# Forget sums by way of device memory and GpSimd's mask instead of TensorE's products, in a two-layer sparse-attention trunk

## The chip, the cores and the metric

The kernel runs on one core of a Trainium2 chip. A core has five engines with their own instruction streams: TensorE (PE; its weight loads are shown apart as PEld), VectorE (DVE), ScalarE (ACT), GpSimd (POOL) and SyncE (SP), which here issues all transfers between device memory and the on-chip memory. The metric is the device time of one execution in microseconds (us), the median of several.

## The reference

Two layers, each a mixing part and a squared-ReLU MLP with sandwich RMSNorm, on 256 tokens of 1024 features. The mixing part has 8 NSA heads (compressed, selected and windowed attention) and 8 FoX heads of 64 features. The change touches the FoX heads alone:

```python
log_f = jax.nn.log_sigmoid(f_logits + f_bias)
cum = jnp.cumsum(log_f, axis=1).transpose(0, 2, 1)
for i in range(s // Q_BLOCK):
    q0, q1 = i * Q_BLOCK, (i + 1) * Q_BLOCK
    logits = (einsum('bhqd,bhkd->bhqk', q[:, :, q0:q1], k[:, :, :q1]) * scale
              + cum[:, :, q0:q1, None] - cum[:, :, None, :q1])
    mask = jnp.arange(q1)[None, :] <= jnp.arange(q0, q1)[:, None]
    p = _masked_softmax(logits, mask)
    outs.append(einsum('bhqk,bhkd->bhqd', p, v[:, :, :q1]))
```

The term that depends on the query alone falls out of the softmax, so a kernel needs only the sum at each key, the same for every query row of a head.

## The kernel before

All 256 tokens are held on chip: features or queries on the 128 partitions (rows of the on-chip memory), two query tiles of 128. Weights stream in once as tiles of up to 512 KB into a ring of raw buffers (`raw`, RBUFS = 8). Each is split into a rounded part `whi` (by ACT, some by POOL) and a remainder `wlo` (by DVE), and products are made as hi·hi, hi·lo and lo·hi. The compression weights of the NSA heads (`w`, from `in_cmp_w_k`, `in_cmp_w_v`) use the same ring without a split.

No order of engines is written out by hand. The Python code calls every operation through a recorder, which keeps the operation with the tiles it reads and writes, gives it a key (its place in the listing, or that of its step in a lane) and an estimated cost, and then plans. The planner goes through a list schedule several times, with due times worked out backwards, tries shifts of the order, judges each plan with simulated lateness, and emits the best: the order of each engine's queue, SP's too, is fixed there. A change of one operation's cost, of a buffer count or of a place in the listing can thus change the order of everything.

The mixing part of a layer runs over 24 entries in steps: 16 NSA entries (pair of heads, parity, selected or windowed branch) at steps 0 to 15, then 8 FoX entries (pair, parity) at steps 16 to 23. At a step, `scores` makes the score products for a pair of heads in one stretch of half-array products (64 of the 128 array rows for each head, side by side) and, per entry and query tile, one DVE instruction that adds a mask from SBUF to the scores in PSUM, writes the result and takes the row minimum of the negated, scaled scores. ACT then exponentiates; the next step scales (by POOL for the windowed branch); a step later TensorE turns the probabilities. Between these, `fill` lists the projection products that keep TensorE busy. Jobs in the list `side` are listed at given steps.

The forget sums: `evac1` turns the gate columns into the tiles `lf` (by `absz` and `minz`). `forget_sums`, at step 13, multiplies `lf` by a triangle of ones (`tri`) in PSUM, ACT copies the result as a rounded part (`cumh`), and two DVE instructions make `cum`, which holds rounded parts and remainders in alternating groups of 32 rows. In `fox_scores`, a product with `selr`, which picks the rows of one head, puts the sums of 384 key columns into the score tile for each of the two heads of a pair, and the key products are added on top. The mask added by DVE is then `causal`, the same for all heads.

```python
nc.tensor.matmul(ps[par][:, 0:384], selr[h, i:i + 1].to_broadcast([HD, P]), T["cum"][h],
                 start=True, stop=False, skip_group_check=True)
nc.vector.tensor_tensor_reduce(
    out=p[:, a:b], in0=ps[t], in1=causal[:, S - (b - a):], op0=OP.add, op1=OP.min, ...)
```

In the trace most instructions carry the line of the emitting loop, so they are told apart by the names of their tiles: `s<-cum,selr` the products of the sums, `s<-fkT,fqT` the key products, `s<-tri,lf` the forget sums, `pr<-s,causal` the masked row minimum, `pr<-pr,st,gate` the scaling on POOL.

Of the kernel before, what the change touches and what calls it, by code (L numbers as in the profile page):

```python
# [18 lines left out]
F32 = mybir.dt.float32  # L19
F32R = mybir.dt.float32r  # L20
AF = mybir.ActivationFunctionType
OP = mybir.AluOpType
PSUM = bass.MemoryType.PSUM

P = 128
D = 1024
# [12 lines left out]
SEQ = range(6, 14), range(4, 12)  # L39
SIDE = (6,11), (4, 9)  # L40
PV1 = 15, 14
AFTER = True
PAIRS = False, False
EVKEY = 1
# [4 lines left out]
XAT, PAT = 2, 9  # L49
FIRSTS = [(0, 1), (1, 2), (2, 3), (3, 4), (4, 5), (5, 6), (6, 8)]  # L50
UPK = 7
TOK, WBUFS, RBUFS = 6, 7, 8
LOAD_LEAD, SPLIT_LEAD = 12, 1
OPERANDS = ("whi", "wlo", "xT", "act0", "act1", "qT", "kx0", "kx1", "raw", "gain", "tok", "rl",
            "pr", "prT", "x0", "x1", "fV", "cum", "cs", "pcT", "vbig", "vS", "vW", "kstk", "kstv", "rT", "rCS")
# [8 lines left out]
SEGS = ((0, 128, 0), (128, 384, 1))  # L64
GELU_C = 1.5957691216057308

C_SID, C_CM, C_M01, C_ROW, C_SEL, C_LOW, C_END = np.cumsum([0, 32, 32, 32, 8, 8, 1]).tolist()


def rotation():  # L70
# [5 lines left out]
def constants():  # L76
    c = np.zeros((P, C_END), np.float32)
    i = np.arange(P)
    for t in range(NT):
        ok = (16 * np.arange(16) + 31)[None, :] <= (i + t * P)[:, None]  # L80
        c[:, C_CM + 16 * t:C_CM + 16 * t + 16] = np.where(ok, 0.0, NEG)
        c[:, C_M01 + 16 * t:C_M01 + 16 * t + 16] = ok
    for h in range(8):
        c[16 * h:16 * h + 16, C_ROW + h] = 1.0
        for r in range(0, P, 32):
            c[r + h, C_SEL + h] = 1.0
    for m in range(32):
        c[m::32, C_SID + m] = 1.0
    c[32:64, C_LOW] = c[96:, C_LOW] = -1.0
    return c  # L90


# [34 lines left out]
class Buf:  # L127


    def __init__(self, pool, shape, dtype, name, tag, bufs, psum):  # L130
        self.pool, self.shape, self.dtype, self.name, self.tag, self.bufs = pool, shape, dtype, name, tag, bufs
        self.psum, self.real = psum, None
        self.size = int(np.prod(shape[1:]))
        self.writes, self.reads, self.ops = [], [], 0


class View:
# [14 lines left out]

    def rearrange(self, pattern, **sizes):
        return self._with(lambda ap: ap.rearrange(pattern, **sizes), ix=_regroup(self.ix, pattern, sizes))

    def to_broadcast(self, shape):
        return self._with(lambda ap: ap.to_broadcast(shape), ix=np.broadcast_to(self.ix, shape[1:]))
# [415 lines left out]
def _cost(op, views):  # L573
    out = op.args[0] if op.args else op.kw["out"]
    n = int(np.prod(out.shape[1:]))
    if op.engine == "sync":
        v = views[0][1]
        return v.shape[0] * int(np.prod(v.shape[1:])) * 4 / 320.0
    if op.engine == "tensor":
        if op.name == "stretch":  # L580
            if op.args[2][0][0] == "transpose":
                return 108.0 * len(op.args[2])

            tiles = [_shape(x[1][1]) for x in op.args[2]]
            return sum((x[1][0].ix.size / (2.4 if x[1][1].dtype == F32R else 0.6) + 20) / (P // min(t))
                       for x, t in zip(op.args[2], tiles)) + RETILE * sum(a != b for a, b in zip(tiles, tiles[1:]))
        if op.name == "transpose":
            return 83.0 if op.args[1].dtype == F32R else 108.0
        if op.args[1].dtype == F32R:
            return 13.6 + n / 2.4  # L590
        return max(220.0, 3 + n / 0.6)
    if op.engine == "gpsimd":
        return {"memset": 150, "affine_select": 250}.get(op.name, 400) + (2.1 if op.name == "tensor_scalar" else 1.0) * n
    if op.engine == "vector":
        if op.name == "reciprocal":
            return 60 + 6.5 * n
        if op.name == "tensor_reduce":
            n = int(np.prod(op.args[1].shape[1:]))
        fast = op.name in ("tensor_copy", "tensor_scalar", "memset") and not any(v.buf.psum for _, v in views)
        aps = sum(isinstance(v, View) for v in op.args[2:4]) if op.name == "tensor_scalar" else int(  # L600
            op.name == "scalar_tensor_tensor" and isinstance(op.args[2], View))
        return 68 + 64 * aps + n * (0.52 if fast else 1.04) + 10 * (op.name == "tensor_tensor_reduce")
    src = op.args[1]
    aps = sum(isinstance(op.kw.get(k), View) for k in ("bias", "scale", "accum_out"))
    return n / 1.2 + (55 if src.buf.psum else 92) + 93 * aps
# [45 lines left out]
def body(tc, A, consts_in, out):  # L651
    with ExitStack() as ctx:

        sb = {False: ctx.enter_context(tc.tile_pool(name="ops", bufs=1))}
        sb[True] = ctx.enter_context(tc.tile_pool(name="sb", bufs=1))
        pp = ctx.enter_context(tc.tile_pool(name="pp", bufs=1, space=PSUM))
        tc.nc.scalar.preload_act_table_set("natural_log_exp_and_others")
        rec = Recorder(tc.nc, tc)
        trunk(rec, A, consts_in, out, sb, pp)
        rec.emit()  # L660


def trunk(nc, A, consts_in, out, sbp, pp):
    def tile(shape, dtype, name, tag=None, bufs=1):
        return nc.tile(sbp[(tag or name) not in OPERANDS], shape, dtype, name, tag, bufs)

# [262 lines left out]
            nc.scalar.activation(hi, xTk[k], AF.Copy, scale=gcol[:, k:k + 1])  # L929
        nc.vector.scalar_tensor_tensor(lo, xTk[k], gcol[:, k:k + 1], hi.bitcast(F32), op0=OP.mult, op1=OP.subtract)  # L930

    selr = tile([P, 8], F32R, name="selr")
    r_mix = [None, None]
    carry = None

    for l in range(DEPTH):
# [190 lines left out]
        def forget_sums():  # L1127

            ps = psum("s")
            nc.tensor.matmul(ps[:, :S], lf[0], ones_low, start=True, stop=False)  # L1130
            nc.tensor.matmul(ps[:, P:S], lf[1], ones_low[:, 0:P], start=False, stop=True)
            top = tile([P, S], F32R, name="cumh", tag="tok", bufs=TOK)
            nc.scalar.activation(top, ps[:, :S], AF.Copy)
            cum = tile([P, 384], F32R, name="cum", tag="cum")
            for o, n in ((0, P), (P, S)):
                nc.vector.scalar_tensor_tensor(cum[:, o:o + n], top[:, :n].bitcast(F32), cst[:, C_LOW:C_LOW + 1], ps[:, :n],
                                               op0=OP.mult, op1=OP.add)
            T["cum"] = cum


        def in_chunk(c, evac):
            n = columns(l, c)[1] - columns(l, c)[0]
# [200 lines left out]
        def fox_scores(pair, then):  # L1343

            ps = [psum("s") for _ in range(2)]
            with nc.stretch():
                for par in range(2):
                    h = slice(par * HD, par * HD + HD)
                    i = 2 * pair + par
                    nc.tensor.matmul(ps[par][:, 0:384], selr[h, i:i + 1].to_broadcast([HD, P]), T["cum"][h],  # L1350
                                     start=True, stop=False, skip_group_check=True)
                for o, n, q0 in ((0, 128, 0), (128, 256, 128)):
                    for par in range(2):
                        h = slice(par * HD, par * HD + HD)
                        nc.tensor.matmul(ps[par][:, o:o + n], T["fqT"][h, pair, q0:q0 + P], T["fkT"][h, pair, 0:n],
                                         start=False, stop=o > 0, skip_group_check=True)
                ov = values(*then) if then else None
            if then:
                o_evac(ov, *then)
            return [(x[:, 0:128], x[:, 128:384]) for x in ps]  # L1360
# [15 lines left out]
        def scores(e):  # L1376
            kind, pair, par, br = e[:4]
            if kind == "fox":
                if par == 0:
                    fill_to(12 + (pair | 1))  # L1380
                    T["sc"] = fox_scores(pair, {0: None if PV1[l] else ("nsa", 1), 1: ("nsa", 3), 3: ("fox", 1)}.get(pair))
                ps = T["sc"][par]
            else:
                if br == 1 and par == 0:
                    fill_to((3, 5, 7, 7)[pair])
                    T["sc"] = nsa_scores(pair)
                ps = T["sc"][par][br - 1]
            p = small([P, 384], "pr", 4)
            st = small([P, 4], "st", 4)
            for a, b, t in SEGS:  # L1390
                nc.vector.tensor_tensor_reduce(
                    out=p[:, a:b], in0=ps[t], in1=causal[:, S - (b - a):], op0=OP.add, op1=OP.min,
                    scale=-0.125, scalar=3.0e38, accum_out=st[:, t:t + 1])
            for a, b, t in SEGS:
                nc.scalar.activation(p[:, a:b], p[:, a:b], AF.Exp, scale=-1.0, bias=st[:, t:t + 1],
                                     accum_out=st[:, 2 + t:3 + t])
            return p, st
# [85 lines left out]
        else:  # L1483

            for n, _ in enumerate(by_token()):
                if n == 6:
                    urgent(carry)
                    next(carry)
                    for t in range(NT):
                        r_mix[t] = rstd_of_x(t, "rm")  # L1490
        if first:
            nc.scalar.activation(selr, cst[:, C_SEL:C_SEL + 8], AF.Copy)
        row_scales()
        kx = [tile([P, 2, S], F32R, name="kx", tag=f"kx{j}") for j in range(2)]
        posT = {"k": rows[:, 0:16], "v": rows[:, 16:32]}
# [6 lines left out]
        if not first:  # L1502
# [12 lines left out]
                (ck + 2, compressed_k), (cv, lambda: (fill_to(("hid", "v")), compressed_exp())),  # L1515
                (cv + 1, lambda: (compressed_scale(), hidden_T("v"))),
                (cv + 2, lambda: (compressed_T(), hidden_gelu("v"))), (cv + 3, compressed_v),
                (13, forget_sums), (18, lambda: fill_to("c5"))]
        prs = {}
        st = {}  # L1520
        pTs = {}
# [236 lines left out]
```

## Time and profile before

| | us |
|---|---|
| median of 3 runs (620.59 to 622.69) | 620.81 |
| profiled execution | 620.68 |
| its span | 618.9 |
| DVE busy | 467.6 |
| ACT busy | 382.2 |
| POOL busy | 55.3 |

The span is the time from the first to the last instruction of the profiled execution; its own time has 1.8 us more around it. Layer 0's attention takes from about 26 to 130 us, its MLP to about 310, layer 1's attention to about 434 and its MLP to the end. The stretch of one MLP, 120 to 320 us, has TensorE busy in 200.00 of 200.00 us.

```profile
120.00:320.00 200.00, 200.00 (x1018) 169.69 (x1015) 142.91 (x212) 112.64 (x174) 0.00 (x0) 1.00 0.55 179
```

After the stretch and its length come the busy time of PE, PEld, DVE, ACT and POOL with their counts of instructions, the granted share of TensorE's clock, the busy share of the DMA engines and the GB/s they moved. In timeline rows the columns are start, length, engine, line and operation; "x6" means that six instructions of one kind are merged in a row.

### The profile page before, as it was taken

Reading aid. Unit: us, or ns where it says so; the run is one execution under the profiler, and the core shown is the slowest. Engines: PE = TensorE matmul, PEld = TensorE weight load, DVE = VectorE, ACT = ScalarE, POOL = GpSimd, SP = SyncE. Lnnn points to the kernel's source line nnn. Section 1 sums busy time; section 2 is a strip of 40 time slices with the busy share of each in tenths; the row PEclk is TensorE's granted clock in tenths of the full one; section 3 lists DMA queues with packets and bytes.
Section 4 is the critical chain, followed back from the end, with each engine's and each line's share of the span. In section 5 each row is a group of like instructions: output and inputs, shape, how many; then the busy total and the mean of one; then the engine's idle time right before and its main releaser. Section 6 shows DMA issues by size and latency. Waiting matters only on the chain.

```text
span 618.9 us, 9911 instructions
## 1 busy us (share of the span) xinstructions
PE 608.3 (98%) x3488; PEld 506.8 (82%) x3488; DVE 467.6 (76%) x1017; ACT 382.2 (62%) x794; POOL 55.3 (9%) x74
## 2 busy tenths in 40 slices
PE   9999999999999999999999999999999999999995
PEld 8877777788888888888888778878888888888884
DVE  7899996689976566566599999685997666566544
ACT  6769976567655556455465798584776455556422
POOL 1246330000000000000002341100000000000000
PEclk9999999999999999999999999999999999999999
DMA  8957765328656656655326549262486556556101
GB/s 291 384 184 272 297 231 166 106 69 283 241 190 203 199 176 203 193 183 181 127 89 218 206 158 341 89 205 68 147 298 204 187 185 202 191 183 203 38 0 68
DMA packets 36274, 115.47 MB, mean 187 GB/s; under 512 B 4576, under 2 KB 6368, under 8 KB 36224
## 3 DMA queue, kind: packets, MB, share of 16 engines
q1 hardware_dynamic: 36224, 114.84, 54.8%
q8 instruction: 27, 0.44, 0.3%
q14 instruction: 23, 0.19, 0.1%
HBM read 113.77 MB, written 1.05 MB: 186 GB/s over the span
## 4 chain that ended last, share of the span: by engine, by line
PE 88%; DVE 6%; POOL 2%; issue 2%; ACT 1%; DVEq 0%; POOLq 0%
PE s L530 35%; PE acc L530 25%; PE x L530 19%; PE o L530 9%; DVE wlo L530 2%; POOL pr L530 1%; DVE m L530 1%; DVE y L530 1%; DVE x L530 1%; DVE pr L530 1%; POOL kstv L530 0%; POOL kstk L530 0%; POOL whi L530 0%; DVE rsqrt L530 0%; ACT kstv L530 0%
## 5 line engine op out<-in xcount | busy, mean ns | idle before, releaser
L530 DVE TENSOR_TENSOR wlo<-wraw,whi 128x1024 fp32r<-128x1024 f32 (+2 forms) x200 | 231.4, 1164 | 93.3 <-ACT whi L530 90.7
L530 ACT ACTIVATE whi<-wraw 128x1024 fp32r<-128x1024 f32 (+4 forms) x190 | 189.4, 1004 | 125.0 <-PE acc L530 60.0
L530 PE MATMUL s<-xT,whi 128*128 128x512 f32 x448 | 112.0, 392 | 0.0
L530 PEld LDWEIGHTS s<-xT,whi 128*128 128x128 f32 x448 | 81.4, 189 | 15.2
L530 PE MATMUL acc<-whi,aT 128*128 128x512 f32 x256 | 88.5, 390 | 0.0
L530 PE MATMUL x<-whi,aT 128*128 128x512 f32 x256 | 88.4, 390 | 0.0
L530 PE MATMUL acc<-xT,whi 128*128 128x512 f32 (+1 forms) x258 | 66.8, 386 | 1.3 <-ACT whi L530 0.6
L530 PEld LDWEIGHTS s<-xT,wlo 128*128 128x128 f32 x448 | 61.1, 190 | 4.4
L530 PE MATMUL s<-xT,wlo 128*128 128x256 f32 x448 | 62.5, 282 | 0.0
L530 ACT ACTIVATE pr<-pr,st 128x256 f32<-128x256 f32 (+1 forms) x128 | 54.8, 447 | 7.4 <-DVE st L530 7.0
L530 PEld LDWEIGHTS acc<-whi,aT 128*128 128x128 f32 x256 | 48.1, 188 | 10.0
L530 PEld LDWEIGHTS x<-whi,aT 128*128 128x128 f32 x256 | 48.1, 188 | 9.7
L530 PEld LDWEIGHTS acc<-xT,whi 128*128 128x128 f32 x258 | 44.1, 190 | 10.4 <-issue 1.7
L530 PE MATMUL x<-wlo,aT 128*128 128x512 f32 x128 | 50.0, 390 | 0.0
L530 PE MATMUL acc<-wlo,aT 128*128 128x512 f32 x128 | 49.9, 390 | 0.0
L530 PE MATMUL acc<-xT,wlo 128*128 128x256 f32 x240 | 39.0, 288 | 0.0
L530 POOL CAST whi<-wraw 128x1024 fp32r<-128x1024 f32 x10 | 12.1, 1208 | 274.6 <-ACT rsqrt L530 239.4
L530 PEld LDWEIGHTS acc<-xT,wlo 128*128 128x128 f32 x240 | 33.6, 189 | 3.1 <-issue 1.4
L530 POOL TENSOR_SCALAR pr<-pr,st,gate 128x128 f32<-128x128 f32 (+1 forms) x32 | 30.0, 944 | 51.2 <-DVE st L530 32.8
L530 ACT ACTIVATE rl<-h 128x512 f32<-128x512 f32 x28 | 17.5, 624 | 19.4 <-DVE h L530 19.4
L530 PEld LDWEIGHTS acc<-wlo,aT 128*128 128x128 f32 x128 | 24.0, 188 | 4.9
L530 ACT ACTIVATE rl<-x 128x512 f32<-128x512 f32 x24 | 14.7, 612 | 21.3 <-PE x L530 16.7
(234 smaller groups left out, 916.5 us busy)
## 6 DMA issues: line engine op xcount, KB each, us to landing
wraw<-in_w_up_dram SPq DMA_DIRECT2D x64, 512.0 KB, 4.2
wraw<-in_w_down_dram SPq DMA_DIRECT2D x64, 512.0 KB, 3.7
wraw<-in_w_fm_dram SPq DMA_DIRECT2D x28, 512.0 KB, 5.1
wraw<-in_w_out_dram SPq DMA_DIRECT2D x16, 512.0 KB, 6.6
wraw<-in_w_dram SPq DMA_DIRECT2D x9, 512.0 KB, 3.5
w<-in_cmp_w_k_dram SPq DMA_DIRECT2D x8, 512.0 KB, 5.2
w<-in_cmp_w_v_dram SPq DMA_DIRECT2D x8, 512.0 KB, 4.2
wraw<-in_w_dram SPq DMA_DIRECT2D x6, 256.0 KB, 4.1
```

Of the source, the lines that this page charges most:

```text
L530: getattr(getattr(self.nc, op.engine), name)(*[real(v) for v in args], **{k: real(v) for k, v in kw.items()})
```

## The change

- `forget_sums` is listed at step 3 (FS) and no longer at 13. ACT copies 8 rows of the sums, in full precision, to a tile, and a DMA stores them (8 heads x 256 keys) to device memory (`fd`).
- `forget_rows` is new, listed once for each pair of heads at steps 9, 11, 17 and 19 (FR). A DMA loads two heads' sums to all 128 rows (`fall`, 2 buffers), and two selections on GpSimd set the keys after the query to the large negative value: one from the first 128 columns to a tile `fdiag` for query tile 0, one in place on the last 128 columns for query tile 1.
- The DVE instruction of a FoX entry adds these tiles, not `causal`.
- The products with `selr`, the tile `cum`, `selr` itself and their constants go.
- The ring of raw weight buffers has 7 places, not 8.
- The planner's cost of a transfer goes by its on-chip side.

```diff
+FS = 3, 3
+FR = 9, 11, 17, 19
-TOK, WBUFS, RBUFS = 6, 7, 8
+TOK, WBUFS, RBUFS = 6, 7, 7
...
-            top = tile([P, S], F32R, name="cumh", tag="tok", bufs=TOK)
-            nc.scalar.activation(top, ps[:, :S], AF.Copy)
-            cum = tile([P, 384], F32R, name="cum", tag="cum")
-            for o, n in ((0, P), (P, S)):
-                nc.vector.scalar_tensor_tensor(cum[:, o:o + n], top[:, :n].bitcast(F32), cst[:, C_LOW:C_LOW + 1], ps[:, :n],
-                                               op0=OP.mult, op1=OP.add)
-            T["cum"] = cum
-
+            row = tokt("cumrow")
+            nc.scalar.activation(row[0:8, 0:S], ps[0:8, :S], AF.Copy)
+            fd = nc.tile(dp, [8, S], F32, "fd", "fd", 2)
+            nc.sync.dma_start(fd, row[0:8, 0:S])
+            T["fd"] = fd
+
+        def forget_rows(pair):
+
+            u = tile([P, 2, S], F32, name="fall", tag="fall", bufs=2)
+            nc.sync.dma_start(u, T["fd"][2 * pair:2 * pair + 2].to_all(P))
+            d = tile([P, 2, P], F32, name="fdiag", tag="fdiag", bufs=2)
+            for dst, c in ((d, slice(0, P)), (u[:, :, P:S], slice(P, S))):
+                nc.gpsimd.affine_select(dst, u[:, :, c], pattern=[[0, 2], [-1, P]], compare_op=OP.is_ge, fill=NEG, base=0,
+                                        channel_multiplier=1)
+            T["fm", pair] = d, u
...
-                for par in range(2):
-                    h = slice(par * HD, par * HD + HD)
-                    i = 2 * pair + par
-                    nc.tensor.matmul(ps[par][:, 0:384], selr[h, i:i + 1].to_broadcast([HD, P]), T["cum"][h],
-                                     start=True, stop=False, skip_group_check=True)
...
-                                         start=False, stop=o > 0, skip_group_check=True)
+                                         start=o == 0, stop=o > 0, skip_group_check=True)
...
-                    out=p[:, a:b], in0=ps[t], in1=causal[:, S - (b - a):], op0=OP.add, op1=OP.min,
+                    out=p[:, a:b], in0=ps[t], in1=T["fm", pair][t][:, par] if kind == "fox" else causal[:, S - (b - a):], op0=OP.add, op1=OP.min,
...
-                (13, forget_sums), (18, lambda: fill_to("c5"))]
+                (FS[l], forget_sums), (18, lambda: fill_to("c5"))]
+        side += [(i, lambda pair=pair: forget_rows(pair)) for pair, i in enumerate(FR)]
```

More of the change, by code (lines that the diff above doesn't have):

```diff
@@ L23 @@
 PSUM = bass.MemoryType.PSUM
+DRAM = bass.MemoryType.DRAM
 P = 128
@@ L65 @@
 GELU_C = 1.5957691216057308
-C_SID, C_CM, C_M01, C_ROW, C_SEL, C_LOW, C_END = np.cumsum([0, 32, 32, 32, 8, 8, 1]).tolist()
+C_SID, C_CM, C_M01, C_ROW, C_END = np.cumsum([0, 32, 32, 32, 8]).tolist()
 def rotation():
@@ L84, in constants @@
         c[16 * h:16 * h + 16, C_ROW + h] = 1.0
-        for r in range(0, P, 32):
-            c[r + h, C_SEL + h] = 1.0
     for m in range(32):
         c[m::32, C_SID + m] = 1.0
-    c[32:64, C_LOW] = c[96:, C_LOW] = -1.0
     return c
@@ L131, in __init__ @@
         self.pool, self.shape, self.dtype, self.name, self.tag, self.bufs = pool, shape, dtype, name, tag, bufs
-        self.psum, self.real = psum, None
+        self.psum, self.dram, self.real = psum, tag[1] == "fd", None
         self.size = int(np.prod(shape[1:]))
@@ L154, in rearrange, with to_all @@
         return self._with(lambda ap: ap.rearrange(pattern, **sizes), ix=_regroup(self.ix, pattern, sizes))
+    def to_all(self, n):
+        return self._with(lambda ap: ap.partition_broadcast(n))
     def to_broadcast(self, shape):
@@ L576, in _cost @@
     if op.engine == "sync":
-        v = views[0][1]
+        v = max((v for _, v in views), key=lambda v: v.buf.dram * 0 if v.buf.dram else v.shape[0] * int(np.prod(v.shape[1:])))
         return v.shape[0] * int(np.prod(v.shape[1:])) * 4 / 320.0
@@ L658, in body, with trunk @@
         rec = Recorder(tc.nc, tc)
-        trunk(rec, A, consts_in, out, sb, pp)
+        dp = ctx.enter_context(tc.tile_pool(name="dp", bufs=1, space=DRAM))
+        trunk(rec, A, consts_in, out, sb, pp, dp)
         rec.emit()
-def trunk(nc, A, consts_in, out, sbp, pp):
+def trunk(nc, A, consts_in, out, sbp, pp, dp):
     def tile(shape, dtype, name, tag=None, bufs=1):
@@ L930, in first_xT @@
         nc.vector.scalar_tensor_tensor(lo, xTk[k], gcol[:, k:k + 1], hi.bitcast(F32), op0=OP.mult, op1=OP.subtract)
-    selr = tile([P, 8], F32R, name="selr")
     r_mix = [None, None]
@@ L1490, in trunk @@
                         r_mix[t] = rstd_of_x(t, "rm")
-        if first:
-            nc.scalar.activation(selr, cst[:, C_SEL:C_SEL + 8], AF.Copy)
         row_scales()
```

## The prediction

> **What bounds the kernel now.** I read the page's span, busy times and chain first, then the table of busy time by stretch over the attention stages, then single groups.
>
> ```profile
> span 618.9 us, 9911 instructions
> PE 608.3 (98%) x3488; PEld 506.8 (82%) x3488; DVE 467.6 (76%) x1017; ACT 382.2 (62%) x794; POOL 55.3 (9%) x74
> PE 88%; DVE 6%; POOL 2%; issue 2%; ACT 1%; DVEq 0%; POOLq 0%
> 40.00:50.00 10.00, 8.97 (x75) 6.29 (x75) 9.32 (x37) 9.83 (x32) 7.85 (x12) 1.00 0.50 177
> 70.00:80.00 10.00, 10.00 (x65) 8.22 (x64) 10.00 (x38) 10.00 (x30) 5.72 (x4) 1.00 1.01 374
> 80.00:90.00 10.00, 9.97 (x81) 7.50 (x80) 10.00 (x38) 6.65 (x21) 2.79 (x3) 1.00 0.79 283
> 90.00:100.00 10.00, 10.00 (x75) 7.48 (x74) 5.57 (x17) 5.42 (x15) 0.00 (x0) 1.00 0.17 53
> 100.00:110.00 10.00, 10.00 (x61) 7.75 (x60) 7.27 (x22) 7.79 (x17) 0.00 (x0) 1.00 0.64 211
> 340.00:350.00 10.00, 9.54 (x80) 7.01 (x79) 9.75 (x40) 8.65 (x31) 4.10 (x10) 1.00 0.27 82
> 400.00:410.00 10.00, 10.00 (x66) 8.53 (x65) 8.73 (x20) 8.79 (x21) 0.00 (x0) 1.00 0.44 141
> ```
>
> The columns of a stretch are its length, the busy time of PE, PEld, DVE, ACT and POOL with instruction counts, the granted clock, the DMA share and GB/s. TensorE is the bound: 98% of the span, 88% of the chain, at the full clock. But the attention stages are not all alike. In the NSA stage (40 to about 85 us in layer 0) DVE and ACT are as full as TensorE, and TensorE has holes: 1.03 of 10 us at 40:50, 0.46 at 340:350. In the FoX stage (from about 85 us, and from 390 us in layer 1) TensorE has no holes, DVE has slack and POOL does nothing. So a product removed from the FoX stage shortens the program by what it holds TensorE for, while work moved into 40:50 or 340:350 may lengthen a hole.
>
> **The change part by part.**
>
> *Products of cum removed.* Each of four head pairs in two layers loses two products (one for each half of the array's rows, side by side) that put the forget sums into PSUM.
>
> ```profile
> 84.80:85.08 0.28, 0.28 (x2) 0.18 (x2) 0.00 (x0) 1.00 0.69 132
> 91.63:91.91 0.28, 0.28 (x2) 0.18 (x2) 0.00 (x0) 1.00 0.00 0
> 104.44:104.71 0.27, 0.27 (x2) 0.18 (x2) 0.00 (x0) 1.00 0.89 364
> sum 2.23, PE 2.23 PEld 1.46 DVE 0.00; mean PE 0.28 PEld 0.18 DVE 0.00
> 49.64 0.63 PE L530 MATMUL s<-kx,qS 64*128 64x256 f32 x6
> 49.86 0.41 PE L530 MATMUL s<-kx,qS 64*128 64x256 f32 x4
> 50.10 0.84 PE L530 MATMUL x<-kx,qS 64*128 64x512 f32 x6
> ```
>
> The first rows are stretches cut from the start of a cum pair to the start of the first key product behind it; the sum is over all eight. So TensorE is held 2.23 us in all. Not all of that goes. The last rows show a score stretch of the NSA heads that also enters from whole-array products: its first pair of 256 columns starts at 49.64, the second at 49.86, the stage's next form at 50.10. The first pair holds TensorE 0.22 us, the other two 0.24 together, 0.12 each: entering the half-array form costs 0.10. The cum pair stands first in its stretch, so the key products inherit that 0.10. What goes is 0.28 - 0.10 = 0.18 a pair by this, or, from the sum, 2.23 - 8 x 0.10 = 1.43 us. The bounds are 1.43 and 2.23; I take **1.4**, since the NSA stretch is the nearest case of the same form. The Trainium skill, "TensorEngine Tiling (Array Packing)", section Tiling Modes, says that changing the tiling mode, and not just the tile, drains the array. By that rule the entry cost stays, as the NSA row has it; without it the sum would be 2.23.
>
> *DVE and ACT work of the sums.* The two DVE instructions that build cum go; ACT's copy shrinks to 8 rows but not in columns, so it stays as long; ACT's one copy of selr goes.
>
> ```profile
> L530 DVE SCALAR_TENSOR_TENSOR cum<-cumh,cst,s x4: 339/408/477, 79.5 to 386.1; 128x256 fp32r<-128x256 f32 x2, 128x128 fp32r<-128x128 f32 x2
> L530 ACT ACTIVATE cumh<-s x2: 365/371/377, 78.1 to 385.0; 128x256 fp32r<-128x256 f32 x2
> L530 ACT ACTIVATE selr<-cst x1: 208/208/208, 26.6 to 26.6; 128x8 fp32r<-128x8 f32 x1
> ```
>
> DVE loses 4 x 0.408 = 1.63 us, in 79.5 to 80.3 and at 386, beside a TensorE that is 9.97 to 10 full there. Between nothing and 1.63 us, I take nothing: TensorE's holes lie earlier. The two-operand add that takes the row minimum keeps its shape and only reads another tile.
>
> *Sums moved from step 13 to step 3.* The matrix products are the same. The chain before them must now be done some 30 us sooner.
>
> ```profile
> 47.38 1.14 PE L530 MATMUL s<-ident,pr 128*128 128x128 f32 x6
> L530 DVE SCALAR_TENSOR_TENSOR absz<-z x4: 146/154/313, 67.4 to 370.1; 128x8 f32<-128x8 f32 x4
> L530 ACT ACTIVATE absz<-absz x4: 192/193/193, 69.1 to 370.6; 128x8 f32<-128x8 f32 x4
> L530 ACT ACTIVATE absz<-absz,one x4: 285/287/293, 69.6 to 372.5; 128x8 f32<-128x8 f32 x4
> L530 DVE TENSOR_SCALAR minz<-z x4: 152/158/294, 67.8 to 370.2; 128x8 f32<-128x8 f32 x4
> L530 DVE SCALAR_TENSOR_TENSOR lf<-absz,minz x4: 159/167/173, 71.0 to 373.3; 128x32 f32<-128x32 f32 x4
> ```
>
> The first row is the turning of the first two probability tiles, which the loop does at steps 2 and 3, so step 3 is near 48 us. A layer has two of each of the other rows: ACT 2 x (0.193 + 0.287) + the copy 0.371 = 1.33 us, DVE 2 x (0.154 + 0.158 + 0.167) = 0.96 us. They leave 67 to 79 us and enter 40 to 48 us, where ACT is busy 9.83 of 10. The bounds are nothing (the planner lets the sums come later, as nothing needs them before the FoX stage) and 1.33 us a layer, 2.7 in all. I take nothing for layer 1, where ACT has 1.35 us free at 340:350, and about 0.3 for layer 0; against that I set the same size for DVE's 1.63 us, of which some may count. Together zero; both ends stay for the range.
>
> *Store, loads and masks.* A layer gains one store of 8 KB, four loads of 256 KB (each two heads' rows, read again for every partition), and eight selections on POOL of 256 elements a row. SP issues them on the one queue that brings the weights, so a wait on SP (for the copied row, for the store, for a free tile) holds the weight loads behind it.
>
> ```profile
> L530 POOL TENSOR_SCALAR_AFFINE_SELECT causal<-causal 128x128 f32<-128x128 f32 x1 | 0.3, 295 | 0.0
> L530 POOL TENSOR_SCALAR pr<-pr,st,gate x32: 446/562/2687, 45.6 to 389.4; 128x128 f32<-128x128 f32 x16, 128x256 f32<-128x256 f32 x16
> PEld s L530 <- POOL pr L530: 0.8, 2, 0.5
> gains<-in_g_post_mix_dram SPq DMA_DIRECT2D x2, 512.0 KB, 8.0
> x<-in_x_dram SPq DMA_DIRECT2D x4, 256.0 KB, 6.2
> out_dram<-x SPq DMA_DIRECT2D x2, 256.0 KB, 2.0
> 71.23 3.12 POOL L530 TENSOR_SCALAR pr<-pr,st,gate 128x256 f32<-128x256 f32 x2 [2.27 <-DVE lf L530]
> 72.44 1.21 DVE L530 TENSOR_TENSOR wlo<-wraw,whi 128x1024 fp32r<-128x1024 f32 x1
> ```
>
> A selection of 128 elements took 0.295 us, so one of 256 is between 0.295 and, by POOL's slowest instruction, 2.69 us; I take 0.59. All this hides if it ends before the row minimum that reads it. The gains load is the nearest to the new ones (one row read for all partitions, twice the bytes): 8.0 us to landing. For the first pair: 2.0 for the store, 8.0 for the load, at worst 2 x 2.69 for the masks, 15.4 us, against 84.80 - 47.38 = 37 us from step 3 to the first scores at step 16. Steps are thus 2.9 us apart, and the load listed at step 9 has 7 x 2.9 = 20 us for its 13.4. For pair 2, whose tile must first be free of pair 0, there are 104.44 - 84.80 = 20 us less the few that pair 0 reads. So these cost nothing; without the cover a pair would cost up to 13 us once.
>
> *Weight buffers, 8 to 7.* SP waits for a free buffer all through; the question is whether one buffer less makes a load late.
>
> ```profile
> 39.03 0.33 SPq L530 DMA_DIRECT2D wraw<-in_w_fm_dram  x1
> 45.43 0.81 SPq L530 DMA_DIRECT2D w<-in_cmp_w_v_dram  x2
> DMA to landing us min/median/max: 4.3/4.3/4.3
> 48.13 1.04 POOL L530 CAST whi<-wraw 128x1024 fp32r<-128x1024 f32 x1
> 49.31 0.39 PE L530 MATMUL acc<-xT,whi 128*128 128x512 f32 x1
> ```
>
> This is the tightest place. The load at 39.03 (landed 4.3 us later, at 43.3) took the last free buffer; the next came free at 45.43. With seven it waits until then: 6.4 us later, against 48.13 - 43.3 = 4.8 us of slack before the split. That is 1.6 us late at worst, if nothing is reordered; the four buffers held by compression weights landed long before use, so their loads can go behind it. Bounds 0 and 1.6 a layer; I take 0.
>
> **Sum.** -1.4 + 0 + 0 + 0. The profiled execution took 620.68 us, 1.8 more than its span and within 0.13 of the median of 620.81. So 620.7 - 1.4 = **619.3 us**, 0.2% less.
>
> **The rivals.**
>
> *The holes close too, or the entry goes with the products* (faster). For it: DVE is full at 70:90 and loses 1.63 us; 2.23 instead of 1.43. Against it: TensorE hardly waits there. 620.7 - 2.23 - 1.63 = 616.8 us.
>
> *The early chain stretches the holes.* For it: ACT 9.83 of 10 at 40:50. Against it: nothing forces the chain early but the order in which products are listed. 619.3 + 1.3 = 620.6, or 622.0 with both layers.
>
> *The masks hold POOL up.* At 71.23 POOL's product took most of 3.12 us beside DVE's subtraction of two SBUF tiles at 72.44. Four selections a layer fall in the NSA stage; each at 2.69 is 0.42 longer than the 2.27 us of idle time that row shows, and delays a gate product by as much, which TensorE then waits for: 8 x 0.42 = 3.4, so 622.7 us. Against it: TensorE waited for POOL just 0.8 us in this stage. The Trainium skill, "GPSIMD Engine Reference", section Key points, says that GpSimd shares its SBUF interfaces with VectorE and contends with instructions of two SBUF inputs; the pair of rows agrees.
>
> *The seventh buffer is missed* (slower). SP reaches the load of 39.03 at 45.43, its split is late, TensorE waits 1.6 us in each layer: 619.3 + 3.2 = 622.5 us, slower than before. It decides as soon as the lateness over both layers passes 1.4 us. If a second load of each layer is late as well, 625.7. Against it: the planner knows the count of buffers and can move the compression weights back.
>
> **Chances.** Forecast 0.55, holes closed 0.14, early chain 0.12, POOL 0.07, buffers 0.12. About 0.5%, 3.1 us, is what a measurement of this kernel can tell from no change: faster means under 617.7, slower over 623.9. Faster: most of the second case and the low edge of the first, 0.15. Slower: half the buffer case and a few hundredths of POOL's and the chain's, 0.10. Within: 0.75. The range leaves out below 617.0 and above 622.7, about 0.1 at each end.
>
> **What would show it.** Right: no row s<-cum,selr; the first key pair of a FoX stretch holding TensorE 0.1 us longer than the second of its size; every selection over before its row minimum; TensorE still 10 of 10 in the FoX stages. Wrong: TensorE under 8.97 of 10 in the stretch that was 40:50 (chain or buffer: ACT's rows or a DMA before the split tell which), DVE waiting for POOL's masks, or POOL's gate products on the chain for more than 2%. A planner that orders all else anew could shift either layer by more than any term here; that would make the sum wrong with its terms right.

## The result, and the profile after

The changed kernel took 618.19 us (median of 5 runs, 618.00 to 618.59) against 621.13 us for the kernel before in the same runs: a ratio of 0.9948 with an interval of 0.9933 to 0.9964. It is faster by about 2.9 us, or 0.5%. The forecast was 1.4 us faster, so the time lies in the range but the gain is twice the one worked out. The profiled executions, 620.68 and 618.19 us, are 2.5 us apart, their spans 2.4. One execution of the changed kernel with a fourth seed took 689.45 us at a granted clock of 0.823, where all others had 0.996 to 0.999; it stands in no median or ratio below.

The page of the changed kernel, then its busy time by stretch, with the same columns as before:

```profile
span 616.5 us, 9921 instructions
PE 606.8 (98%) x3472; PEld 506.3 (82%) x3472; DVE 466.6 (76%) x1013; ACT 381.3 (62%) x793; POOL 65.0 (11%) x90
PE 88%; DVE 8%; ACT 2%; issue 1%; POOL 0%; DVEq 0%
fall<-fd SPq DMA_DIRECT2D x8, 256.0 KB, 4.3
```

```profile
40.00:50.00 10.00, 9.74 (x82) 7.01 (x80) 9.32 (x40) 9.47 (x32) 5.31 (x9) 1.00 0.79 300
90.00:100.00 10.00, 10.00 (x80) 7.59 (x79) 6.61 (x23) 5.66 (x16) 1.31 (x4) 1.00 0.52 167
340.00:350.00 10.00, 9.79 (x81) 7.06 (x80) 10.00 (x46) 8.71 (x33) 4.87 (x7) 1.00 0.22 74
400.00:410.00 10.00, 10.00 (x72) 7.68 (x71) 8.08 (x25) 8.11 (x25) 0.77 (x2) 1.00 0.44 139
```

TensorE has 16 instructions fewer, the products with `selr`, and POOL 16 more, the selections. TensorE is still the bound, and the FoX stages stayed full. The stretch 40:50 lost 0.26 us of 10, where it had lost 1.03. POOL's share of the chain fell from 2% to 0%, although it works longer. Over a whole attention stage, the first row for layer 0 and the second for layer 1, first before, then after:

```profile
26.00:128.00 102.00, 100.29 (x684) 77.68 (x682) 88.49 (x281) 73.36 (x207) 30.63 (x33) 1.00 0.59 208
312.00:434.00 122.00, 121.22 (x842) 99.36 (x841) 107.41 (x326) 85.63 (x235) 21.77 (x29) 1.00 0.51 174
```

```profile
26.00:128.00 102.00, 100.21 (x684) 78.22 (x684) 89.38 (x282) 73.89 (x206) 30.98 (x41) 1.00 0.62 216
312.00:434.00 122.00, 121.79 (x840) 99.59 (x839) 108.41 (x326) 86.73 (x239) 31.69 (x37) 1.00 0.54 182
```

TensorE's holes are 1.71 and 0.78 us before, 1.79 and 0.21 after. So in layer 0 they only moved (30:40 now loses 1.00 us of 10, where it had lost 0.25), and in layer 1 they shrank by 0.57.

Where along the program the time went can be read from work that both programs do at the same place: the last down products of layer 0's MLP on TensorE, and the last writes of the result by DVE. First before, then after:

```profile
309.51 0.39 PE L530 MATMUL acc<-whi,aT 128*128 128x512 f32 x1
614.05 1.54 DVE L530 SCALAR_TENSOR_TENSOR x<-m,rsqrt,x 128x512 f32<-128x512 f32 x3
```

```profile
308.82 0.39 PE L533 MATMUL acc<-whi,aT 128*128 128x512 f32 x1
612.09 1.54 DVE L533 SCALAR_TENSOR_TENSOR x<-m,rsqrt,x 128x512 f32<-128x512 f32 x3
```

The first is 0.69 us earlier, the second 1.96. So layer 0 gave 0.69 us, layer 1 gave 1.27, and the last 0.5 us of the spans' difference lies behind the last writes. There both programs do the same work, the stores of the result. First before, then after:

```profile
609.45 6.68 SPq L530 DMA_DIRECT2D out_dram<-x  x6
```

```profile
607.48 6.69 SPq L533 DMA_DIRECT2D out_dram<-x  x6
```

The last store's issue ends at 616.13 us of a span of 618.9 before, and at 614.17 of 616.5 after. The end of the program follows it by 2.8 us and by 2.3, although the stores land 1.7 to 2.1 us after their issue in both.

What the FoX pairs themselves gave is seen from stretches that begin with the first half-array product of each pair and end with the first product behind the last. The first row of eight and their sum, before and then after:

```profile
84.80:85.82 1.02, 1.02 (x11) 0.69 (x10) 1.02 (x4) 0.00 (x0) 0.45 (x1) 1.00 0.88 273
...
sum 8.21, PE 8.21 PEld 5.56 DVE 6.75 ACT 3.50 POOL 0.45; mean PE 1.03 PEld 0.70 DVE 0.84 ACT 0.44 POOL 0.06
```

```profile
85.52:86.38 0.86, 0.86 (x10) 0.53 (x9) 0.86 (x2) 0.86 (x3) 0.86 (x1) 1.00 1.04 426
...
sum 6.84, PE 6.84 PEld 4.19 DVE 4.95 ACT 5.18 POOL 1.35; mean PE 0.85 PEld 0.52 DVE 0.62 ACT 0.65 POOL 0.17
```

They hold TensorE 8.21 - 6.84 = 1.37 us less, 0.69 in layer 0 and 0.68 in layer 1. With the 0.5 us less of holes over both layers and the 0.5 at the end, this makes up the 2.4 us between the spans to within 0.1. The pairs are half of the 2.9 us. The experiments ask whether this half is what it seems, and where the other half comes from.

### The profile page after: what moved, and what is told of

Its sections match the earlier page's. It is cut to its first block, busy times and chain, and to the rows that moved or that the text cites. A ratio compares the mean times of both kernels' runs of the same rounds, so it can differ in the third digit from the quotient of the medians.

```text
span 616.5 us, 9921 instructions
## 1 busy us (share of the span) xinstructions
PE 606.8 (98%) x3472; PEld 506.3 (82%) x3472; DVE 466.6 (76%) x1013; ACT 381.3 (62%) x793; POOL 65.0 (11%) x90
## 4 chain that ended last, share of the span: by engine, by line
PE 88%; DVE 8%; ACT 2%; issue 1%; POOL 0%; DVEq 0%
PE s L533 35%; PE acc L533 26%; PE x L533 20%; PE o L533 8%; DVE wlo L533 2%; DVE m L533 1%; DVE y L533 1%; DVE x L533 1%; ACT pr L533 0%; DVE mg L533 0%; DVE rsqrt L533 0%; POOL pr L533 0%; DVE xT L533 0%; DVE rCS L533 0%; DVE pr L533 0%
## 5 line engine op out<-in xcount | busy, mean ns | idle before, releaser
L533 ACT ACTIVATE pr<-pr,st 128x128 f32<-128x128 f32 (+1 forms) x128 | 55.1, 447 | 5.6 <-DVE st L533 5.4
L533 POOL TENSOR_SCALAR pr<-pr,st,gate 128x256 f32<-128x256 f32 (+1 forms) x32 | 30.9, 975 | 47.1 <-DVE st L533 36.8
```

The lines of the kernel that those rows point to most:

```text
L533: getattr(getattr(self.nc, op.engine), name)(*[real(v) for v in args], **{k: real(v) for k, v in kw.items()})
```

## The experiments

Ratios are to the kernel before, run on the same chip, with the interval in brackets. Since any edit of the listing makes the planner order everything anew, some experiments keep a plan and edit only what is written out from it, and others keep the work and change only the plan.

### The products alone, plan kept

```diff
+                begun = set()
                 for name, args, kw in op.args[2] if op.name == "stretch" else [(op.name, op.args, op.kw)]:
+                    if name == "matmul" and args[2].buf.name == "cum":
+                        begun.add(args[0].buf)
+                        continue
+                    if args and isinstance(args[0], View) and args[0].buf in begun:
+                        begun.discard(args[0].buf)
+                        kw = dict(kw, start=True)
```

> The kernel before with its own plan, every queue in the same order, but the sixteen products of cum with selr are left out when the program is written, so the forget sums do not enter the scores. Theory (products net of the entry into the half-array form): the time falls by 8 x 0.17 = 1.4 us, to about 619.7 beside 621.1, and the first key pair of each FoX stretch holds TensorE about 0.1 us longer than in the kernel before. Rival (the entry goes too): it falls by 2.2 us, to 618.9. Rival (TensorE's time in the FoX stage is hidden): it falls by less than 0.4 us.

619.69 us, 0.9974 (0.9964 to 0.9983): 1.6 us faster (1.1 to 2.2). The stretches of its eight FoX pairs:

```profile
84.99:85.85 0.86, 0.86 (x10) 0.53 (x9) 0.86 (x4) 0.00 (x0) 0.46 (x1) 1.00 0.83 231
...
sum 6.86, PE 6.86 PEld 4.21 DVE 5.61 ACT 3.23 POOL 0.46; mean PE 0.86 PEld 0.53 DVE 0.70 ACT 0.40 POOL 0.06
```

8.21 - 6.86 = 1.35 us, as in the changed kernel. The hidden case is out, and by the stretches the 2.23 us of the gross case too. The time of the whole agrees, though its interval alone could not tell 1.4 from 2.2.

### The products and DVE's and ACT's part, plan kept

```diff
             for op in self.order():
+                if op.args and isinstance(op.args[0], View) and op.args[0].buf.name in ("cum", "cumh", "selr"):
+                    continue
...
```

The dots stand for the same test on the buffers and the edit of the run before it.

> As the run before it, same plan, and also without the four DVE instructions that build cum, the two ACT copies to cumh and the one to selr; the forget sums do not enter the scores. Theory (DVE's share lies beside a full TensorE): within 0.4 us of the run with only the products left out. Rival (freed DVE closes TensorE's holes): 1.0 to 1.6 us less than that run.

620.04 us, 0.9978 (0.9969 to 0.9987). No gain over the run before it: with the queues' order fixed, 1.63 us less of DVE are worth nothing that can be measured, and the rival that has them close holes falls for this plan.

### The products put back into the changed kernel, plan kept

```diff
...
+                if op.name == "stretch" and parts[0][1][1].buf.name == "fqT":
+                    fed = [parts[0][1][0].buf, parts[1][1][0].buf]
+                    for par, o in enumerate(fed):
+                        h = slice(par * HD, par * HD + HD)
+                        self.nc.tensor.matmul(o.real[:, 0:384], zero[h, :], both[h, 0].rearrange("p j n -> p (j n)")[:, 0:384],
+                                              start=True, stop=False, skip_group_check=True)
...
```

> The changed kernel with its own plan, and two products of a zero tile with 384 columns put back ahead of the key products of each FoX pair when the program is written (the result is the same; two small instructions at the start make the zeros). Theory (products net of the entry are 1.4 us of the change): 618.2 + 1.4 = 619.6 us. Rival (they explain the whole change): 621.1 us. Rival (the gain is the new plan's alone): 618.2 us.

619.38 us, 0.9963 (0.9950 to 0.9975): 1.2 us more than the changed kernel, by medians. The two intervals overlap, so whole times alone do not show the difference. Its eight stretches:

```profile
85.38:86.41 1.03, 1.03 (x12) 0.70 (x11) 1.03 (x2) 1.03 (x3) 1.03 (x1) 1.00 1.08 384
...
sum 8.24, PE 8.24 PEld 5.58 DVE 6.02 ACT 6.08 POOL 1.35; mean PE 1.03 PEld 0.70 DVE 0.75 ACT 0.76 POOL 0.17
```

8.24 against 6.84: the same 1.4 us from the other side, by the stretches. With the products back, the changed kernel is still 2.0 us faster by medians than the kernel before (621.37 in these runs). That part is not the products.

### Seven buffers alone, planned anew

```diff
-TOK, WBUFS, RBUFS = 6, 7, 8
+TOK, WBUFS, RBUFS = 6, 7, 7
```

> The kernel before, planned anew with 7 raw weight buffers in place of 8, nothing else. Theory (the planner moves the compression weights back and nothing becomes late): 621.1 us within 0.6. Rival (the load that took the eighth buffer is 1.6 us late in each layer): 622.7 to 624.3 us.

619.67 us, 0.9964 (0.9952 to 0.9977): 1.7 us faster by medians, 2.2 by the ratio, with all products in place. Neither expectation holds. One buffer less can hardly speed up a transfer, so the next question was how far plans differ among themselves.

### Other seeds of the planner

The planner's trials draw from a generator with a fixed seed; another seed gives another plan of the same work.

```diff
-        rng = np.random.default_rng(1)
+        rng = np.random.default_rng(2)
```

The kernel before with seeds 2 and 3:

> The kernel before, unchanged but for the seed of the planner's random trials, so another plan of the same work. Theory (the plan alone moves the time by more than a microsecond): between 619 and 623 us, and not the same as 621.4. Rival (plans are all alike): 621.4 within 0.5.

> As the run before it with a third seed. Same expectations: by the theory 619 to 623 us, and one of the two differs from 621.4 by over 1 us; by the rival both are 621.4 within 0.5.

The kernel before with 7 buffers and seeds 2 and 3:

> The kernel before with 7 raw buffers and the second seed. Theory (the 1.7 us that 7 buffers gained with the first seed was the luck of a new plan): no steady gain over the 8-buffer kernel of the same seed, 619 to 623 us. Rival (7 buffers are better in themselves): 1 to 2 us less than the 8-buffer kernel of the same seed.

> As the run before it with the third seed. Theory: no steady gain over 8 buffers of the same seed, 619 to 623 us. Rival: again 1 to 2 us less.

The changed kernel with seeds 2, 3 and 4:

> The changed kernel with the planner's second seed. Theory (the change is worth 1.4 us for its products, and the rest of its gain belongs to the plan, which spreads by 2 to 5 us): anywhere from 616 to 622 us, the mean of the changed kernel's seeds 1 to 3 about 1.4 us under that of the kernel before and its two other seeds (620.9), so about 619.5. Rival (the change as a whole is worth 2.9 us in any plan): 618.2 within 0.6.

> As the run before it with the third seed. Theory: 616 to 622 us. Rival: 618.2 within 0.6.

> As the run before it with a fourth seed. Theory: 616 to 622 us. Rival: 618.2 within 0.6.

| work | seed | median us | ratio |
|---|---|---|---|
| before, 8 buffers | 2 | 620.96 | 1.0001 (0.9991 to 1.0010) |
| before, 8 buffers | 3 | 620.64 | 0.9993 (0.9984 to 1.0002) |
| before, 7 buffers | 1 | 619.67 | 0.9964 (0.9952 to 0.9977) |
| before, 7 buffers | 2 | 617.61 | 0.9945 (0.9930 to 0.9960) |
| before, 7 buffers | 3 | 623.10 | 1.0033 (1.0020 to 1.0045) |
| changed | 1 | 618.19 | 0.9948 (0.9933 to 0.9964) |
| changed | 2 | 619.48 | 0.9973 (0.9963 to 0.9983) |
| changed | 3 | 618.30 | 0.9959 (0.9946 to 0.9973) |
| changed | 4 | 618.44 | 0.9958 (0.9942 to 0.9973) |

Several expectations of mine fell. The plans of the kernel before with 8 buffers lie within 0.5 us of each other, where I had looked for one more than 1 us off. The mean of the changed kernel's seeds 1 to 3 is 618.7 us, not 619.5; seeds 3 and 4 lie within 0.6 of 618.2, as the rival of a steady gain has it, and only seed 2 does not. There was no steady gain from 7 buffers (seed 2 took 3.4 us less than 8 buffers of the same seed, seed 3 took 2.5 more), but both times lie outside the 619 to 623 us that I had given, and the three plans with 7 buffers lie 5.5 us apart: the best is as fast as the changed kernel, products and all; the worst is 2.0 us slower than the kernel before. The difference is in TensorE's holes. The attention stages of both layers in the best and then the worst of the three:

```profile
26.00:128.00 102.00, 101.99 (x701) 80.23 (x700) 90.46 (x288) 76.08 (x209) 24.09 (x33) 1.00 0.59 209
312.00:434.00 122.00, 121.31 (x844) 99.32 (x842) 107.05 (x325) 87.12 (x239) 23.97 (x29) 1.00 0.50 171
```

```profile
26.00:128.00 102.00, 99.46 (x686) 78.08 (x685) 88.08 (x282) 72.37 (x205) 20.76 (x33) 1.00 0.59 208
312.00:434.00 122.00, 119.01 (x828) 96.82 (x827) 107.68 (x321) 82.59 (x232) 22.09 (x29) 1.00 0.50 174
```

The holes are 0.01 + 0.69 = 0.70 us in the first and 2.54 + 2.99 = 5.53 in the second. The difference of 4.8 is most of the 5.5. The longest waits of TensorE in the two stages of the worst one, the first in layer 0 and the second in layer 1, are these (total, times, longest):

```profile
PE acc L530 <- ACT whi L530: 1.2, 1, 1.2
PE s L530 <- DVE pb L530: 1.2, 1, 1.2
```

These are a split that ACT made late and a short DVE chain of the compression. No row of its waits has TensorE wait for a DMA. That the order of the queues made them late is the likely reading, as the work is the same, but no run shows it by itself.

### The sums listed later

```diff
-FS = 3, 3
-FR = 9, 11, 17, 19
+FS = 10, 10
+FR = 13, 14, 17, 19
```

> The changed kernel with the forget sums listed at step 10 and the first two pairs' loads at 13 and 14 (not 3, 9 and 11), planned anew with the first seed. Theory (the early chain costs nothing, the plan's spread does the rest): within the spread of the four plans of the changed kernel, 618.2 to 619.5 us. Rival (the early chain stretches the holes at 40 to 50 us): 616.0 to 617.3 us, as 1.3 to 2.7 us come back. Rival (the masks then come too late or hold POOL up beside the last NSA entries): over 620 us.

618.46 us, 0.9958 (0.9945 to 0.9972), amid the other four plans of the changed kernel. In this run the chain ahead of the sums starts at 57.0 us, in the changed kernel at 39.1:

```profile
L533 DVE SCALAR_TENSOR_TENSOR absz<-z x4: 139/152/154, 57.0 to 359.1; 128x8 f32<-128x8 f32 x4
```

```profile
L533 DVE SCALAR_TENSOR_TENSOR absz<-z x4: 152/156/221, 39.1 to 341.7; 128x8 f32<-128x8 f32 x4
```

A place 18 us earlier or later is worth nothing that shows above the spread of plans.

## Why the prediction was right, and where its size was not

**Products removed: right, in mechanism and size.** Worked out as 2.23 - 8 x 0.10 = 1.43 us, measured as 1.37, 1.35 and 1.40 us in the stretches of three programs, and as 1.6 and 1.2 us in whole times with the plan kept. That the key products inherit the entry is seen in the changed kernel, where a window behind its first pair shows when the second one starts:

```profile
85.52 0.93 PE L533 MATMUL s<-fkT,fqT 64*128 64x128 f32 x8
85.74 0.50 PE L533 MATMUL s<-fkT,fqT 64*128 64x128 f32 x4
```

The first pair holds TensorE for 0.22 us. In the kernel before, the same pair, behind cum, held it 0.11, as the two rows here show:

```profile
85.08 0.82 PE L530 MATMUL s<-fkT,fqT 64*128 64x128 f32 x8
85.19 0.49 PE L530 MATMUL s<-fkT,fqT 64*128 64x128 f32 x4
```

The range of 617.0 to 622.7 us also holds the unchanged 620.7, so that the time lies in it says little; these stretches carry the mechanism.

**DVE's and ACT's work, and the sums moved: right as taken.** Taken together as zero; the runs that test them, one for each, show nothing beyond the scatter.

**Store, loads and masks: right that they cost nothing, with less room than claimed.** The rows of the changed kernel:

```profile
L533 POOL TENSOR_SCALAR_AFFINE_SELECT fdiag<-fall x8: 403/407/1445, 59.5 to 403.4; 128x256 f32<-128x256 f32 x8
L533 POOL TENSOR_SCALAR_AFFINE_SELECT fall<-fall x8: 403/408/1392, 59.8 to 403.1; 128x256 f32<-128x256 f32 x8
DMA to landing us min/median/max: 3.4/4.3/4.5
```

A selection took 0.41 us (I took 0.59), at worst 1.45 (I bounded by 2.69); a load 4.3 us, not the 8.0 of the gains. The cover held with the least room at pair 2 of layer 1, whose load could go only when pair 0 had been read:

```profile
393.27 0.34 SPq L533 DMA_DIRECT2D fall<-fd  x1
396.85 1.45 POOL L533 TENSOR_SCALAR_AFFINE_SELECT fdiag<-fall 128x256 f32<-128x256 f32 x1 [7.04 <-DMA fall<-fd]
398.25 0.40 POOL L533 TENSOR_SCALAR_AFFINE_SELECT fall<-fall 128x256 f32<-128x256 f32 x1
401.67 0.49 PE L533 MATMUL s<-fkT,fqT 64*128 64x128 f32 x4
```

The masks were ready at 398.65 us, 3.0 before this pair's score products began. The prediction had read some 20 us between pairs 0 and 2 from layer 0. Here there were 401.67 - 390.63 = 11.0 us, less than the 13.4 that its worst prices for a load and two masks add up to. So the cover did not have the room that was claimed; it held because the load and the masks were cheaper.

The rival that has the masks hold POOL up fell. TensorE's one wait for a gate product of POOL in the changed kernel took 0.5 us (0.2 before) and lay at 55.7 us, ahead of the first mask at 59.45. Three of the 16 selections did start within a DVE subtraction of two SBUF tiles and took 1.39 to 1.45 us, the other 13 took 0.40 to 0.51. One of the three:

```profile
59.81 1.39 POOL L533 TENSOR_SCALAR_AFFINE_SELECT fall<-fall 128x256 f32<-128x256 f32 x1
```

```profile
59.60 1.34 DVE L533 TENSOR_TENSOR wlo<-wraw,whi 128x1024 fp32r<-128x1024 f32 x1
```

The Trainium skill, "GPSIMD Engine Reference", section Key points, names DVE instructions with two SBUF inputs among those that contend for the shared SBUF interfaces; these rows agree.

**Weight buffers: the bound was wrong.** It read "Bounds 0 and 1.6 a layer; I take 0". It asked only whether a load would be late under the order of the kernel before, and so bounded the edit at zero from below. No row has TensorE wait for a load. But a new count of buffers makes the planner order the whole attention stage anew, and three such plans gave -1.7, -3.5 and +2.0 us (by medians). The closing caution, that the planner "could shift either layer by more than any term here", was true, yet the sum gave it no term and the range reached only as far as the priced rivals.

**What the sum left out.** It was short by 1.5 us. In the two profiled executions the rest of the gain is the 0.5 us less of holes and the 0.5 us at the end. The end is no scatter. From the last store's issue to the end of the program it takes 2.8 to 2.9 us in all eight traces of the kernel before and its variants (other seeds, 7 buffers, products left out, DVE's and ACT's part left out), and 2.3 us in all six of the changed kernel and its variants (products put back included). So it is not made by the products, nor by DVE's and ACT's part of the sums, nor by the seven buffers, but by something else in the change. Which part does, no row shows.

The five plans of the changed kernel (four seeds and the later listing) have a mean ratio of 0.9959, the three of the kernel before 0.9998: the change is worth 0.0039 x 621.1 = 2.4 us on average over plans, the plan that was timed 0.5 to 0.8 us more than that. Of the 2.4, the products are 1.4 and the end 0.5. **The last 0.5 us stays open.** TensorE's holes in the two attention stages sum to 1.8 to 3.2 us (mean 2.5) in the three plans before and 1.6 to 3.2 (mean 2.2) in the five after, so a better order after the change is not shown. Nor is a gain from 7 buffers: the mean of the three plans with them, 0.9981, would cover it, but with a spread of 5.5 us between them it proves nothing, and no run has the changed kernel with 8.

The prediction drew its bound for "faster" at 617.7 us and gave 0.75 to a time within its bounds. 618.19 us is within, but narrowly: as a ratio, the gain of 0.36% to 0.67% lies on both sides of the 0.5% that the bound stood for. The 0.10 for slower did not follow from the prices: the buffer case at 622.5 us lies under the 623.9 that was to count as slower.

No version was measurably faster than the changed kernel: the old work with 7 buffers and seed 2 (0.9930 to 0.9960) cannot be told from it (0.9933 to 0.9964).

## What to carry to other kernels

On a full TensorE, price a removed product by the time until the next product starts, and take off what the next one then pays itself: here a first product of a half-array stretch pays 0.10 us for the change of form, whoever is first. Where a planner orders the queues, time several seeds of both kernels before calling a gain of a microsecond the edit's own, and test the edit under a kept plan by changing only what is written out from it. A sum of terms read from one plan leaves out what a new plan does by itself: the spread between plans belongs in the range. And account for the whole span, its end too: here 0.5 us of the gain lay behind the last write, where no term of the sum looked.

## What the runs showed of the hardware that was not expected

A load that reads 2 KB of device memory again for each of 128 rows (256 KB in all) landed in 3.4 to 4.5 us, like a weight load of twice the bytes (medians of 3.4 to 4.3 us for most weights on the same page) and not like the 8.0 us of the gains load. The two loads of that group were issued at 72.5 and 380.5 us, in stretches with a DMA share of 1.01 and 0.86, the new ones in stretches of 0.45 to 0.87. Whether that makes the difference is not shown. And GpSimd's selection over 256 columns took 0.41 us against 0.295 over 128, so doubling the width cost 0.11 us, not 0.295.
